# Two decoder layers on one core: the second layer's mixing gate and channel-mixing modulation are summed during the first layer's output projection and upward product

## The chip, the cores and the metric

The kernel runs on one core of one Trainium2 chip. The time is device time in microseconds of one execution, the median of the runs; lower is better. The engines of the core are TensorE (PE), VectorE (DVE), ScalarE (ACT), GpSimd (POOL) and SyncE (SP), which issues nearly all transfers. Each engine runs its own instructions in the order in which they were put, and waits for others by semaphores.

## The reference

Two layers (DEPTH = 2) over 1024 positions of width 1024, in float32. A vector `c` gives six modulation vectors per layer, 1024 long each: shift, scale and gate for token mixing, and the same for channel mixing.

```python
c_act = jax.nn.silu(c)
for l in range(DEPTH):
    mod = c_act @ ada_w[l] + ada_b[l]
    shift_m, scale_m, gate_m, shift_f, scale_f, gate_f = split(mod, 6)
    h = rms_norm(x, g_pre_mix[l]) * (1.0 + scale_m) + shift_m
    proj = h @ w_in[l] + b_in[l]
    # sliding-window attention with sinks, and a causal pooling mixer, on columns of proj
    ...
    y = concat([attention, pooled]) @ w_out[l]
    x = x + gate_m * rms_norm(y, g_post_mix[l])
    h = rms_norm(x, g_pre_ffn[l]) * (1.0 + scale_f) + shift_f
    y = (silu(h @ w_gate[l]) * (h @ w_up[l])) @ w_down[l]
    x = x + gate_f * rms_norm(y, g_post_ffn[l])
```

The change concerns `gate_m`, `scale_f` and `shift_f` of the second layer. They depend on `c` and the weights alone, so they may be worked out at any time before the second layer uses them.

## The kernel before

**Number format.** Every large product runs as three TensorE products of rounded high and low parts (`mm3`, lines L263, L266, L267; in `double` of the products by pairs the same lines). `split` makes the parts: ACT rounds (L220, high), DVE subtracts (L221, low). A matmul takes a 128x128 left operand and 512 columns. Results go to PSUM banks `acc`, of which there are four.

**Stages of a layer.** Positions are halved (512 each), and a half has four tiles of 128. Per layer: mixing (input projection, attention and pooling of both halves; in it the output projection of the first half, out0, and six first products of the channel mixing), then out1, the output projection of the second half, then `firsts[1]` (the first products of eight column pairs), then ups, and down. out0 and out1 are `natural_proj` (L664): two column halves, in each 8 k-steps of 12 matmuls, and at the end of a half four DVE products L691 that empty the four banks. The next half needs the banks again.

**ups** works through 11 pairs of columns (`up_pair`, L1137), each with products named T2, T3, T1, B22, T4 (a product for two banks is 24 matmuls). Their left operands are sums of weight quarters on DVE: L1177, L1178 (the left of T2), L1182, L1183 (the left of T3). Each bank's result is added to another by L1162 on DVE. L1099, L1196, L1198, L1200, L1207 finish the pair's SwiGLU rows. The weights come by four transfers of line L1145 per pair, on SP, two to a tile `raw`.

**Modulation jobs.** A job (`ada_sum`, L285) makes 512 numbers of a modulation vector: eight weight tiles of 128x512 (256 KB each, L306, SP) come into the buffers `ar`, of which there are two, and DVE sums them, each scaled by a column of `c_act`, into `ada` (L296 the first, L298 the other seven). The sum over partitions is then taken by PE, in one of three ways:
- `ada_gate` (L457): the sum is split into `ph` high and low parts, and two matmuls with a picking column (L469, L470) give one row of 512. DVE adds the bias and multiplies by a gain (L471, L472, in place in two `ar` buffers), and L473 stores it to DRAM; `load_gate` loads it when needed. Two jobs per sub-layer.
- `ada_pair` (L404): also split; two picking matmuls per job (L412, L413) collect four jobs in one bank of four rows, which ACT copies (L417) and PE transposes (L420); L424 adds the bias.
- `ada_columns` (L435): no split; four fp32 matmuls of the sum against a column of ones (L441) give columns at once, L446 adds the bias, L400 finishes the scale. Four jobs per sub-layer.

A job is a generator of five steps (ADA = 5): four that load two tiles each and sum the two before them, and a last one. `run(stream, steps, (other, n), ...)` steps through a main stream and takes n steps of the others spread evenly over it. Where a step of another stream stands among the main stream's instructions settles the order on each engine, within what the scheduler then moves.

**Where the jobs run before.** `ada_jobs(l)` (L1447): two gate jobs and four `ada_pair` jobs of channel mixing, in the mixing stage of the layer that uses them. The channel mixing's gate, two jobs of `ada_gate(l, 1)`, runs during ups, 14 steps over 55. The second layer's shift and scale of mixing, four `ada_columns` jobs, run during the first layer's down. out1 has no job beside it.

Of the kernel before, what the change touches and what calls it, by code (L numbers as in the profile page):

```python
# [23 lines left out]
DEPTH = 2  # L24
# [12 lines left out]
NPAIR = NFF // 2  # L37
KD = D // P
# [28 lines left out]
def hybrid_decoder_kernel(  # L67
# [367 lines left out]
    def ada_columns(l, sub, cols, ab):  # L435


        def close(r, acc):
            bank = msc_bank()
            for i in range(4):  # L440
                nc.tensor.matmul(  # L441
                    bank[:, i : i + 1], acc[:, i * P : (i + 1) * P], ones[:, 0:1], start=True, stop=True
                )
            m, o = r // 2, slice(r % 2 * 4, r % 2 * 4 + 4)
            k0 = (3 * sub + 1 - m) * KD
            nc.vector.tensor_add(ab[:, m, o], bank[:, 0:4], cols[:, k0 + o.start : k0 + o.stop])  # L446
            if m == 0:
                ada_scale(ab, sub, o, cols)

        return [  # L450
            (l, (3 * sub + 1 - r // 2) * D + r % 2 * 512, lambda acc, r=r: close(r, acc), True)
            for r in range(4)
        ]
# [3 lines left out]
    def ada_gate(l, sub):  # L457

        gates[l, sub] = row = dr.tile([1, D], F32, tag="gate", name="gate", bufs=2 * DEPTH)

        def close(half, hi, lo):
            n0 = (3 * sub + 2) * D + half * 512
            o = slice(half * 512, half * 512 + 512)
            gb = t_("ar", [P, 512])[0:1]
            gg = t_("ar", [P, 512])[0:1]
            nc.sync.dma_start(gb, ada_b[l : l + 1, n0 : n0 + 512])
            nc.sync.dma_start(gg, (g_post_ffn if sub else g_post_mix)[l : l + 1, o])
            bank = msc_bank()
            nc.tensor.matmul(bank[0:1, :], picks[:, 3:4], hi, start=True, stop=False)  # L469
            nc.tensor.matmul(bank[0:1, :], picks[:, 3:4], lo, start=False, stop=True)  # L470
            nc.vector.tensor_add(gb, bank[0:1, :], gb)  # L471
            nc.vector.tensor_mul(gb, gb, gg)  # L472
            nc.sync.dma_start(row[:, o], gb)  # L473

        return [
            (l, (3 * sub + 2) * D + half * 512, lambda hi, lo, half=half: close(half, hi, lo))
            for half in range(2)
        ]
# [6 lines left out]
    ADA = KD // 2 + 1  # L485

    def ada_stream(jobs):

        for l, n0, close, *whole in jobs:
            got = []  # L490
            yield from ada_sum(l, n0, got, *whole)
            close(*got)
# [869 lines left out]
    def layer_cols(l, rows=None):  # L1362
        return dict(cols=cols_of(rows or load_col_rows(l)), abm=t_("colp", [P, 2, KD]), abf=t_("colp", [P, 2, KD]))
# [81 lines left out]

    rotary_tables(recent["cast"])
    def ada_jobs(l):  # L1447
        return ada_stream(ada_gate(l, 0) + ada_pair(l, 1, par["cols"], par["abf"]))

    FIRST = (3, NPAIR - 3)  # L1450
    for l in range(DEPTH):
        cols = par["cols"]
# [21 lines left out]
        side = ada_jobs(l)  # L1474
# [52 lines left out]
        drain(pool)  # L1527
        xs = load_residual(1)
        fn, ss, out1 = mix_out(l, cats[1], G)
        for i, _ in enumerate(out1, 1):  # L1530
            if i == 2 * KD:
                next(firsts[1])

        def second_norm():
            yield from post_norm(1, fn, ss, xs)
# [11 lines left out]
        run(firsts[1], 2 * FIRST[1], (norm, NT + 2 + HK + 2))  # L1547
        drain(norm)

        nxt, jobs = None, []  # L1550
        if l + 1 < DEPTH:
            nxt = layer_cols(l + 1)
            jobs = ada_columns(l + 1, 0, nxt["cols"], nxt["abm"])
        side = ada_stream(ada_gate(l, 1))

        wd, load = down_loads(l)

# [5 lines left out]
                        after(load(B11, g), recent["raw"])  # L1563
                    yield

        run(ups(), 5 * NPAIR + 2 * (NPAIR - sum(FIRST)), (side, 2 * ADA + 4))
        drain(side)
        G = load_gate(l, 1)
        side = ada_stream(jobs)
# [91 lines left out]
```

## Time and profile before

| what | value |
|---|---|
| median of 3 runs | 1906.01 us (1905.44 to 1906.4) |
| the profiled execution's span | 1904.4 us |
| first layer's mixing | 50 to 309 us |
| first layer's out1, firsts[1], ups, down | 309 to 356, 356 to 437, 437 to 745, 745 to 990 us |
| second layer's mixing | 990 to 1246 us |
| second layer's out1, firsts[1], ups, down | from 1246, 1293, 1374 and 1682 us to the end |

The profile shows one execution. The times of the stages are read from the first and last instructions of their lines in the timeline. In a row of the view by windows, a number with (x...) is an engine's busy time and its instructions. In the timeline a row is start, duration, engine, line and operation, output and inputs; `[0.33 <-ACT hi L220]` is idle time of the engine just before the row, and what ended it. Rows of waits give the sum, the number and the longest.

### The profile page before, as it was taken

Reading aid. Unit: us, or ns where it says so; the run is one execution under the profiler, and the core shown is the slowest. Engines: PE = TensorE matmul, PEld = TensorE weight load, DVE = VectorE, ACT = ScalarE, POOL = GpSimd, SP = SyncE. Lnnn points to the kernel's source line nnn. Section 1 sums busy time; section 2 is a strip of 40 time slices with the busy share of each in tenths; the row PEclk is TensorE's granted clock in tenths of the full one; section 3 lists DMA queues with packets and bytes.
Section 4 is the critical chain, followed back from the end, with each engine's and each line's share of the span. In section 5 each row is a group of like instructions: output and inputs, shape, how many; then the busy total and the mean of one; then the engine's idle time right before and its main releaser. Section 6 shows DMA issues by size and latency. Waiting matters only on the chain.

```text
span 1904.4 us, 26019 instructions
## 1 busy us (share of the span) xinstructions
PE 1864.7 (98%) x8954; PEld 1540.3 (81%) x8954; DVE 1540.4 (81%) x2889; ACT 948.4 (50%) x1791; POOL 20.0 (1%) x67
## 2 busy tenths in 40 slices
PE   7999999999999999999999999999999999999998
PEld 5887788888888788888888868888887888888886
DVE  7899886668898888788879988846888888867687
ACT  4875795654222223445558667845622222234452
POOL 0000000000000000000000000000000000000000
PEclk9999999999999999999999989999999999999999
DMA  9345563655555665944554464536654565574343
GB/s 341 112 144 161 161 221 125 191 172 193 194 183 188 205 210 172 320 143 150 172 179 139 126 181 164 178 111 209 214 189 146 198 216 197 199 249 157 117 141 114
DMA packets 229540, 341.86 MB, mean 180 GB/s; under 512 B 17016, under 2 KB 126472, under 8 KB 229408
## 3 DMA queue, kind: packets, MB, share of 16 engines
q1 hardware_dynamic: 228800, 338.10, 53.8%
q10 hardware_dynamic: 576, 2.10, 0.3%
q8 instruction: 70, 1.15, 0.3%
q14 instruction: 62, 0.51, 0.1%
q0 software_dynamic: 32, 0.00, 0.0%
HBM read 267.25 MB, written 72.89 MB: 179 GB/s over the span
## 4 chain that ended last, share of the span: by engine, by line
PE 80%; DVE 10%; DMA 5%; ACT 3%; issue 2%; SPq 0%; DVEq 0%; ACTq 0%; POOL 0%; POOLq 0%
PE acc L263 25%; PE acc L266 24%; PE acc L267 24%; DMA ar<-in_ada_w_dram 2%; DVE lo L221 1%; DVE ada L298 1%; DMA raw<-in_w_up_dram 1%; PE msc L904 1%; PE msc L561 1%; ACT hi L220 1%; PE pv L263 1%; PE pv L266 1%; PE pv L267 1%; ACT raw L554 1%; DVE fn L1162 1%
## 5 line engine op out<-in xcount | busy, mean ns | idle before, releaser
L220 ACT ACTIVATE hi<-raw 128x1024 fp32r<-128x1024 f32 (+1 forms) x388 | 331.8, 868 | 360.1 <-PE acc L266 197.1
L221 DVE TENSOR_TENSOR lo<-raw,hi 128x1024 fp32r<-128x1024 f32 (+1 forms) x388 | 380.2, 987 | 121.3 <-ACT hi L220 116.4
L263 PE MATMUL acc<-t,hi 128*128 128x512 f32 x704 | 274.6, 390 | 2.7 <-ACT hi L220 2.6
L266 PE MATMUL acc<-t,hi 128*128 128x512 f32 x704 | 274.0, 389 | 0.0
L267 PE MATMUL acc<-t,lo 128*128 128x512 f32 x704 | 271.8, 389 | 0.0
L263 PE MATMUL acc<-bh,hi 128*128 128x512 f32 x520 | 202.8, 390 | 0.0
L267 PE MATMUL acc<-bh,lo 128*128 128x512 f32 x520 | 202.4, 389 | 0.0
L263 PE MATMUL acc<-hT,hi 128*128 128x512 f32 x480 | 190.2, 396 | 0.6 <-DVE fn L691 0.6
L266 PE MATMUL acc<-hT,hi 128*128 128x512 f32 x480 | 188.4, 392 | 0.0
L267 PE MATMUL acc<-hT,lo 128*128 128x512 f32 x480 | 187.6, 392 | 0.0
L1162 DVE TENSOR_TENSOR fn<-acc,fn 128x512 f32<-128x512 f32 x220 | 150.3, 685 | 38.2 <-PE acc L267 37.6
L263 PEld LDWEIGHTS acc<-t,hi 128*128 128x128 f32 x704 | 132.2, 188 | 32.1 <-ACT hi L220 5.1
L267 PEld LDWEIGHTS acc<-t,lo 128*128 128x128 f32 x704 | 132.2, 188 | 28.7 <-DVE lo L221 1.2
L266 PEld LDWEIGHTS acc<-t,hi 128*128 128x128 f32 x704 | 132.2, 188 | 27.1
L266 PE MATMUL acc<-ph,hi 128*128 128x512 f32 x320 | 124.7, 390 | 0.0
L1098 ACT ACTIVATE fn<-fn 128x512 f32<-128x512 f32 x44 | 27.9, 633 | 181.7 <-DVE fn L1162 181.7
L263 PEld LDWEIGHTS acc<-bh,hi 128*128 128x128 f32 x520 | 97.6, 188 | 20.2
L267 PEld LDWEIGHTS acc<-bh,lo 128*128 128x128 f32 x520 | 97.6, 188 | 20.2
L298 DVE SCALAR_TENSOR_TENSOR ada<-ar,c_act,ada 128x512 f32<-128x512 f32 x140 | 104.6, 747 | 10.1 <-DMA ar<-in_ada_w_dram 9.7
L263 PE MATMUL acc<-hi 128*128 128x512 f32 x256 | 103.5, 410 | 2.4 <-DVE fn L691 2.0
L263 PEld LDWEIGHTS acc<-hT,hi 128*128 128x128 f32 x480 | 90.2, 188 | 19.2 <-DVE fn L691 1.4
L267 PEld LDWEIGHTS acc<-hT,lo 128*128 128x128 f32 x480 | 90.1, 188 | 18.6 <-issue 0.2
(323 smaller groups left out, 3814.5 us busy)
## 6 DMA issues: line engine op xcount, KB each, us to landing
ar<-in_ada_w_dram SPq DMA_DIRECT2D x160, 256.0 KB
raw<-in_w_gate_dram SPq DMA_DIRECT2D x44, 512.0 KB
raw<-in_w_up_dram SPq DMA_DIRECT2D x44, 512.0 KB
raw<-in_w_in_dram SPq DMA_DIRECT2D x80, 256.0 KB
raw<-keeps SPq DMA_DIRECT2D x40, 512.0 KB
keeps<-fn SPq DMA_DIRECT2D x66, 256.0 KB
two_b<-in_w_down_dram SPq DMA_DIRECT2D x30, 512.0 KB
raw<-keepa SPq DMA_DIRECT2D x25, 512.0 KB
```

The source lines that it names most:

```text
L220: a = nc.scalar.activation(hi, src, AF.Copy)
L221: v = nc.vector.tensor_sub(lo, src, hi.bitcast(F32))
L263: ins = nc.tensor.matmul(dst, lh, rh, start=first, stop=False)
L266: nc.tensor.matmul(dst, lh, rl, start=False, stop=False)
L267: return nc.tensor.matmul(dst, ll, rh, start=False, stop=last)
L298: ins = nc.vector.scalar_tensor_tensor(acc, w, c_act[:, i : i + 1], acc, op0=ALU.mult, op1=ALU.add)
L554: nc.scalar.activation(hf, bank, AF.Identity, bias=shift, scale=scale)
L561: ins = nc.tensor.transpose(bank[:, t * P : (t + 1) * P], src[t], ident)
L904: nc.tensor.transpose(bank[:, i * P : (i + 1) * P], s[:, ii, ck * P : (ck + 1) * P], ident)
L1098: nc.scalar.activation(g, g, AF.Silu)
L1162: nc.vector.tensor_add(halves_of(dst)[m], bank, halves_of(src)[m])
```

## The change

`ada_jobs` makes no jobs for the second layer. During the first layer, the second layer's two gate jobs and four channel-mixing jobs (these as `ada_columns` instead of `ada_pair`) become one stream `ahead`. 15 of its 30 steps run beside the 16 k-steps of the first layer's out1; what is left comes in ups, ahead of the two gate jobs that were there, at 29 steps over 55 in place of 14. `layer_cols` of the second layer (bias and gain columns) moves from ahead of ups to ahead of out1.

```diff
     def ada_jobs(l):
+        if l:
+            return iter(())
         return ada_stream(ada_gate(l, 0) + ada_pair(l, 1, par["cols"], par["abf"]))
...
         fn, ss, out1 = mix_out(l, cats[1], G)
-        for i, _ in enumerate(out1, 1):
-            if i == 2 * KD:
-                next(firsts[1])
+        nxt, ahead = None, iter(())
+        if l + 1 < DEPTH:
+            nxt = layer_cols(l + 1)
+            ahead = ada_stream(ada_gate(l + 1, 0) + ada_columns(l + 1, 1, nxt["cols"], nxt["abf"]))
+
+        def out1_ahead():
+            for i, _ in enumerate(out1, 1):
+                if i == 2 * KD:
+                    next(firsts[1])
+                yield
+
+        run(out1_ahead(), 2 * KD, (ahead, 3 * ADA))
...
-        nxt, jobs = None, []
-        if l + 1 < DEPTH:
-            nxt = layer_cols(l + 1)
-            jobs = ada_columns(l + 1, 0, nxt["cols"], nxt["abm"])
-        side = ada_stream(ada_gate(l, 1))
+        jobs = ada_columns(l + 1, 0, nxt["cols"], nxt["abm"]) if nxt else []
+
+        def ups_side():
+            yield from ahead
+            yield from ada_stream(ada_gate(l, 1))
+
+        side = ups_side()
...
-        run(ups(), 5 * NPAIR + 2 * (NPAIR - sum(FIRST)), (side, 2 * ADA + 4))
+        run(ups(), 5 * NPAIR + 2 * (NPAIR - sum(FIRST)), (side, (5 if nxt else 2) * ADA + 4))
```

The order of instructions shows three places. First, DVE at the boundary between the two column halves of the first layer's out1, before:

```order
L221 TENSOR_TENSOR lo<-cfb,hi 128x512
L221 TENSOR_TENSOR lo<-raw,hi 128x512 x2
L691 TENSOR_TENSOR fn<-acc,G 128x512 x3
L221 TENSOR_TENSOR lo<-raw,hi 128x512
L691 TENSOR_TENSOR fn<-acc,G 128x512
```

and after, from the first gate job's last operations on (`ar<-msc,ar` is its bias, L296 the first tile of the second gate job):

```order
L471 TENSOR_TENSOR ar<-msc,ar 1x512
L221 TENSOR_TENSOR lo<-raw,hi 128x512
L472 TENSOR_TENSOR ar<-ar 1x512
L221 TENSOR_TENSOR lo<-raw,hi 128x512
L691 TENSOR_TENSOR fn<-acc,G 128x512 x2
L296 TENSOR_SCALAR ada<-ar,c_act 128x512
L691 TENSOR_TENSOR fn<-acc,G 128x512
L221 TENSOR_TENSOR lo<-raw,hi 128x512
L691 TENSOR_TENSOR fn<-acc,G 128x512
```

The third and the fourth L691 now stand behind a first sum that needs a loaded tile. At the end of out1 it is the same with L296 ahead of all four and an L298 between the second and the third.

Second, DVE in the second pair of the first layer's ups, from the eviction L1162 of T4's first bank (the pair before) on, before (`lo<-raw,hi` is first the split of T2's left operand, then T3's):

```order
L1162 TENSOR_TENSOR fn<-acc,fn 128x512
L1196 TENSOR_TENSOR sb<-fn,sb 128x512
L1183 TENSOR_TENSOR raw<-raw 128x8x128
L1198 TENSOR_TENSOR fn<-sb,sa 128x512
L1200 TENSOR_TENSOR fn<-sa,fn 128x512
L1162 TENSOR_TENSOR fn<-acc,fn 128x512
L221 TENSOR_TENSOR lo<-raw,hi 128x1024
L1099 TENSOR_TENSOR fn<-fn 128x512
L1162 TENSOR_TENSOR fn<-acc,fn 128x512
L1207 TENSOR_TENSOR fn<-fn 128x512
```

and after:

```order
L1162 TENSOR_TENSOR fn<-acc,fn 128x512
L1196 TENSOR_TENSOR sb<-fn,sb 128x512
L298 SCALAR_TENSOR_TENSOR ada<-ar,c_act,ada 128x512
L1198 TENSOR_TENSOR fn<-sb,sa 128x512
L1200 TENSOR_TENSOR fn<-sa,fn 128x512
L1162 TENSOR_TENSOR fn<-acc,fn 128x512
L298 SCALAR_TENSOR_TENSOR ada<-ar,c_act,ada 128x512
L1099 TENSOR_TENSOR fn<-fn 128x512
L1162 TENSOR_TENSOR fn<-acc,fn 128x512
L1207 TENSOR_TENSOR fn<-fn 128x512
L1183 TENSOR_TENSOR raw<-raw 128x8x128
L1162 TENSOR_TENSOR fn<-acc,fn 128x512
```

In these rows the first two L1162 belong to the two banks of T4 of the pair before, and the third to the first bank of this pair's T2. L1183, the sum that T3 needs, stood third and now stands behind that L1162. It is so in the second, fourth, fifth, seventh and tenth pair; in the sixth, eighth and ninth T2's own split L221 stands behind T4's second L1162. Before, L1183 stood ahead of all L1162 of T2 in every pair.

Third, SP in ups, where the weight loads of a pair (L1145) stand; before, in the third pair's loads:

```order
L1145 DMA raw<-in_w_gate_dram 128x4x256
L306 DMA ar<-in_ada_w_dram 128x512
L1145 DMA raw<-in_w_up_dram 128x4x256
L306 DMA ar<-in_ada_w_dram 128x512
L1151 DMA fn<-firsts 128x1024
L1145 DMA raw<-in_w_gate_dram 128x4x256
L1145 DMA raw<-in_w_up_dram 128x4x256
```

and after, in the loads of a pair in the middle of ups:

```order
L1145 DMA raw<-in_w_gate_dram 128x4x256
L306 DMA ar<-in_ada_w_dram 128x512
L1145 DMA raw<-in_w_up_dram 128x4x256
L306 DMA ar<-in_ada_w_dram 128x512
L1151 DMA fn<-firsts 128x1024
L1145 DMA raw<-in_w_gate_dram 128x4x256
L306 DMA ar<-in_ada_w_dram 128x512 x2
L1145 DMA raw<-in_w_up_dram 128x4x256
```

Before, two L306 at most stood among a pair's loads, and in many pairs none; now up to four do, and two or three in most pairs. In the second layer's mixing no operation of the jobs is left, and its out1, ups and down stand as before.

## The prediction

> **What bounds the kernel now.** I read the head of the page first, then TensorE's share and clock by slices.
>
> ```profile
> span 1904.4 us, 26019 instructions
> PE 1864.7 (98%) x8954; PEld 1540.3 (81%) x8954; DVE 1540.4 (81%) x2889; ACT 948.4 (50%) x1791; POOL 20.0 (1%) x67
> PEclk9999999999999999999999989999999999999999
> ```
>
> TensorE (PE) sets the end: it is busy 98% of the span, at full clock in all slices but one. So the change can gain only where PE waits or is slowed, and loses wherever it makes PE wait. That slice is the second layer's mixing. The view by windows gives the stages that the change touches: time, then busy us of PE, PEld, DVE, ACT, POOL, then PE's clock, DMA share and GB/s.
>
> ```profile
> 309.00:356.00 47.00, 46.71 (x205) 37.85 (x204) 22.81 (x35) 23.96 (x46) 0.00 (x0) 1.00 0.33 102
> 356.00:437.00 81.00, 81.00 (x375) 67.39 (x374) 60.77 (x103) 49.27 (x82) 0.00 (x0) 1.00 0.68 216
> 437.00:745.00 308.00, 306.68 (x1351) 252.36 (x1350) 260.67 (x335) 83.46 (x97) 0.00 (x0) 1.00 0.54 184
> 990.00:1095.00 105.00, 103.36 (x669) 90.33 (x668) 96.02 (x294) 76.73 (x192) 3.59 (x11) 1.00 0.43 133
> 1095.00:1150.00 55.00, 50.85 (x238) 38.88 (x236) 47.12 (x130) 33.36 (x82) 0.70 (x1) 0.91 0.60 179
> 1150.00:1230.00 80.00, 78.45 (x447) 66.31 (x447) 66.09 (x184) 68.84 (x165) 2.73 (x8) 1.00 0.52 172
> ```
>
> In order: first layer's out1, firsts[1] and ups; then second layer's mixing in three stretches, of which only the last holds no modulation work. Where the six jobs are taken from, PE idles 4.15 of 55 us and the clock is 0.91; where they are put, PE loses 0.29, 0.00 and 1.32 us. DVE is the engine to watch: in out1 it is half free (22.81 of 47), in ups it is busy 260.67 of 308.
>
> **What goes, from the second layer's mixing.** The waits of PE in the middle stretch are two of the jobs' making, and the DVE rows from there show how: each L298 adds one weight tile into a modulation sum, each L691 frees a PSUM bank of out0.
>
> ```profile
> PE msc L825 <- DVE rt L798: 1.6, 1, 1.6
> PE acc L263 <- DVE fn L691: 1.2, 2, 0.8
> ...
> 1128.88 1.28 DVE L691 TENSOR_TENSOR fn<-acc,G 128x512 f32<-128x512 f32 x2
> 1130.08 0.74 DVE L298 SCALAR_TENSOR_TENSOR ada<-ar,c_act,ada 128x512 f32<-128x512 f32 x1
> 1130.74 0.68 DVE L691 TENSOR_TENSOR fn<-acc,G 128x512 f32<-128x512 f32 x1
> 1131.35 0.75 DVE L298 SCALAR_TENSOR_TENSOR ada<-ar,c_act,ada 128x512 f32<-128x512 f32 x1
> 1132.01 0.68 DVE L691 TENSOR_TENSOR fn<-acc,G 128x512 f32<-128x512 f32 x1
> ```
>
> I price the waits against the stretch without jobs, which idles 1.55 of 80 us, 1.9%. At that share the 55 us would idle 1.1 instead of 4.15: 3.1 us. The clock of 0.91 costs 55 x 0.09 = 5.0 us of full-speed work. The stretch 990 to 1095 idles 1.6%, so nothing is to be had there. The matmuls that leave are 12: eight picks matmuls of `ada_pair` and four of `ada_gate`. Their pitch, and the four transposes:
>
> ```profile
> 531.39 0.39 PE L266 MATMUL acc<-t,hi 128*128 128x512 f32 x1
> 531.62 0.39 PE L267 MATMUL acc<-t,lo 128*128 128x512 f32 x1
> ...
> 1144.21 0.34 PE msc L420 x4
> ```
>
> Starts lie 0.23 us apart (a record's 0.39 overlaps the next), so 12 x 0.23 + 0.34 = 3.1 us. The term is **-11.2 us** (3.1 + 5.0 + 3.1). Its lower end is -5 (other waits of that stage, which the third stretch also has, take the place of half), its upper end -15 (all idle time of the first two stretches, 1.64 + 4.15, with clock 5.0 and matmuls 3.1, is 13.9, and small gaps between records on top).
>
> **What comes, in out1.** Both gate jobs and the first tiles of the third now run here, 15 steps over 16 k-steps. DVE has room: 22.81 us plus 14 L298 and 2 L296, about 10 us, in 47. Four picks matmuls arrive: 4 x 0.23 = 0.9. They stand in the middle of a k-step and wait for the split of the sum; the like waits of the pair's matmuls (L412) were these:
>
> ```profile
> its engine sat idle before it (us, times) until:
>   ACT ph L220: 0.5, 2
> ```
>
> I take 0.5 us for each of two, 1.0. At both bank boundaries of out1 the changed order puts an L296 or L298 ahead of some of the four L691, and L296 waits for its tile. A tile takes this long, by the chain of waits in the second layer:
>
> ```profile
> 1109.27 4.01 DMA ar<-in_ada_w_dram
> ...
> 1115.42 3.07 DMA ar<-in_ada_w_dram
> ```
>
> Its `ar` slot becomes free at the gate's L472, two k-steps (5.5 us) before the boundary less some 2 us for the picks, so a 4-us load lands about when L296 stands first: 0.9 us for the first boundary, 0.7 (one L298) for the second. The term is **+3.5 us**, from +1 (everything hidden, matmuls alone) to +7.5 (each boundary waits out one more load of 3 to 4 us less what has gone by). firsts[1] takes the rest of the third job, some five L298 on a DVE with 20 us to spare: **+0.5**, 0 to 2. I cost the second layer's `layer_cols`, which now stands ahead of out1, at nothing: a few small rows beside out1's DMA share of 0.33; without that cover it would be one load, 4 us.
>
> **What comes, in ups.** Four column jobs close here, on top of the two gate jobs that were here before. Where `ada_pair` made one row set for four jobs, `ada_columns` runs four fp32 matmuls per job (L441). The same line runs in the first layer's down stage:
>
> ```profile
> 786.36 0.39 PE L267 MATMUL acc<-bh,lo 128*128 128x512 f32 x1
> 786.59 0.94 PE L441 MATMUL msc<-ones_r,ada 128*128 128x1 f32 x8
> 787.40 0.49 PE L263 MATMUL acc<-bh,hi 128*128 128x512 f32 x1
> ```
>
> From 786.59 to 787.40 is 0.81 us; four jobs cost **+3.2**, with PE full on both sides of it.
>
> DVE gets 24 more tile sums (three of the four jobs) of 0.67 us, 16 us, and its idle time of 47 us covers them on average. Not in place, though. Each pair's T3 needs the sum L1183, then ACT's rounding; L1183's start to T3's start is this long in the trace:
>
> ```profile
> 531.25 1.22 DVE L1183 TENSOR_TENSOR raw<-raw 128x1024 f32<-128x1024 f32 x1
> 532.39 0.68 DVE L1207 TENSOR_TENSOR fn<-fn 128x512 f32<-128x512 f32 x1
> 532.99 0.68 DVE L1162 TENSOR_TENSOR fn<-acc,fn 128x512 f32<-128x512 f32 x1
> ...
> 532.98 0.39 PE L267 MATMUL acc<-t,lo 128*128 128x512 f32 x1
> 533.70 0.50 PE L263 MATMUL acc<-t,hi 128*128 128x512 f32 x1 [0.33 <-ACT hi L220]
> ```
>
> 2.45 us (531.25 to 533.70), and PE lost 533.70 - 532.98 - 0.23 = 0.49 there. The other pair in which a job's L298 pushed L1183 late lost 1.15:
>
> ```profile
> 642.97 0.39 PE L267 MATMUL acc<-t,lo 128*128 128x512 f32 x1
> 644.35 0.50 PE L263 MATMUL acc<-t,hi 128*128 128x512 f32 x1 [0.99 <-ACT hi L220]
> ```
>
> These two, 1.64 us, were all of it, since L1183 stood ahead of every eviction of T2. In the changed order the added operations push it further: in five of the pairs (second, fourth, fifth, seventh, tenth) L1183 stands **behind the first L1162 of T2**, and that one can't start before T2's first bank is finished. An eviction starts 0.43 us after the start of its bank's last matmul:
>
> ```profile
> 513.94 0.39 PE L267 MATMUL acc<-t,lo 128*128 128x512 f32 x1
> 514.37 0.69 DVE L1162 TENSOR_TENSOR sb<-acc,fn 128x512 f32<-128x512 f32 x1 [0.63 <-PE acc L267]
> ```
>
> So with L1162 and L1207 ahead (0.60 each, start to start) T3 starts 0.43 + 1.20 + 2.45 = 4.08 after that matmul, while PE has T2's second bank, 13 pitches, 2.96 us. PE loses 1.1; with an L298 between as well, 1.8; with L1207 gone by, 0.5. The five pairs: 1.1 + 1.8 + 1.1 + 0.5 + 1.8 = 6.3. In three other pairs (sixth, eighth, ninth) T2's own split L221 stands behind the second L1162 of T4: 0.43 + 0.60 + 1.2 for the split is 2.2 us, against 4 matmuls and one pitch, 1.1: PE loses 1.1 twice, and 2.4 in the ninth, where an L298 and L1099 stand between too. Together 4.6. The stalls are 6.3 + 4.6 = 10.9, less 1.64 before: **+9.3**. They are counted from PE's own matmuls, so a DVE that is otherwise early can't remove them; the lower bound is +6 (orders ahead with less width), the upper +12 (DVE behind from the pair before).
>
> Whether such stalls cost clock too is open. Two windows show a stall and what followed:
>
> ```profile
> 1095.00:1100.00 5.00, 3.27 (x17) 2.34 (x15) 4.92 (x20) 2.62 (x7) 0.00 (x0) 1.00 0.57 155
> 1100.00:1105.00 5.00, 4.82 (x18) 3.86 (x19) 4.45 (x10) 3.77 (x8) 0.00 (x0) 0.66 0.49 141
> ```
>
> After the 1.6-us wait the clock was 0.66 for 5 us, 1.7 us of work lost. After the 1.15-us stall in ups none was (clock 1.00 in its window). Of the three stalls of 1.8 and 2.4 us I count one as followed by a drop: **+1.7**, 0 to 5.1.
>
> Here a rule of the Trainium skill speaks otherwise ("TensorE: Matmul & The Clock Gate", "What's actually happening"): it gives the half clock only after an idle window of about 3.4 us. By it no stall here would cost clock, and the sum would be 1.7 us less; the trace disagrees, with 0.66 after a wait of 1.6 us, so I keep the term.
>
> **Sum.** -11.2 + 3.5 + 0.5 + 3.2 + 9.3 + 1.7 = +7.0 us on the execution of 1904.4. The runs' median, 1906.0, is 1.6 above the span: 1904.4 + 7.0 + 1.6 = **1913.0 us**. A measurement here can tell about 0.2%, 3.8 us, from no change: bounds 1902.2 and 1909.8.
>
> **The rivals.**
>
> *Not slower: DVE sets the pace of the whole second-layer mixing.* It is busy 96.02 of 105 and 47.12 of 55 us there, 91% and 86%, and loses this:
>
> ```profile
> 437.00:745.00 308.00, 10.44 (x14) 1.00 0.54 184
> 990.00:1230.00 240.00, 31.43 (x42) 0.98 0.50 156
> ```
>
> (L298 alone: busy and count in ups, then in the second layer's mixing.) Of 31.4 us, DVE's idle time there (8.98 + 7.88 = 16.9) already covers some, 14.5 would come off, with 3.1 of matmuls: -17.6 in place of -11.2. The clock's 1.7 may go as well: 7.0 - 6.4 - 1.7 = -1.1, **1905 us**. It decides from a relief of 14.4 us on: there the sum falls under +3.8. Against it: PE is busy 103.36 of 105 in the first stretch, so DVE isn't waited for there. It passes below 1902 only from a relief of 22. Chance 0.25, of which 0.08 below 1902.2.
>
> *Heavier: weight loads held on SP.* In ups a pair's four weight loads were issued almost free of modulation loads; now up to two L306 stand between the two halves of one tile, and L306 waits for a slot that an L298 frees. T2 starts from those loads:
>
> ```profile
> DVE raw L1177 <- DMA raw<-in_w_up_dram: 2.9, 4, 1.5
> ```
>
> Four waits, the longest 1.5 us, so the loads are not early now. If three pairs come one L306 late, a 3-us transfer less 0.5 of slack, 7.5 us are added: **1920.5 us**. For it: the order. Against it: DMA share is 0.54. Chance 0.20.
>
> *The change doesn't do what it says:* the jobs could spill past ups, where everything waits for the drain. The last L471 stands in the tenth of eleven pairs, so no; chance 0.02, at +4 for one load: 1917.
>
> **Numbers.** Forecast 0.53 at 1913.0 (1908 to 1917), not slower 0.25 at 1905, heavier 0.20 at 1920.5. Range 1901.5 to 1922.5: from the lower ends of all terms (-15 + 1 + 3.2 + 6 = -4.8, 1901.2) to the heavier rival with one more drop of the clock (1922.2). Faster by over 0.2%: 0.08. Within: 0.17 and a tenth of the forecast's own part, some 0.22 in all. Slower: 0.70.
>
> **What would show it.** PE's idle share and clock in the second layer's mixing: 1.9% and 1.00, the stage 11 us shorter. out1 of the first layer 50.5 us instead of 47, ups 322 instead of 308, with waits of PE for ACT's L220 (T3) and for DVE's L221 (T2) in eight pairs, none above 2.6 us. Long waits of L1177 for DMA would speak for the second rival, a mixing stage shorter by over 15 us for the first. The forecast is wrong if ups grows by less than 8 us.

## The result, and the profile after

The changed kernel took 1918.91 us in the median (1916.77 to 1920.1, 4 runs) beside 1906.2 for before: 1.006 times, 95% interval 1.0048 to 1.0073. It is slower, by 9 to 14 us. The page of the changed kernel, lines as shown of before:

```profile
span 1918.3 us, 26041 instructions
PE 1865.5 (97%) x8974; PEld 1540.2 (80%) x8974; DVE 1541.2 (80%) x2888; ACT 943.3 (49%) x1786; POOL 18.9 (1%) x67
PEclk9999999999999999999999999999999999999999
```

PE and DVE did the same work (1865.5 and 1541.2 us busy against 1864.7 and 1540.4) in a span 13.9 us longer, so the time went into waits. The view by windows shows where (columns as in the prediction; the stages lie up to 25 us later than in before):

```profile
309.00:360.00 51.00, 49.02 (x214) 38.70 (x213) 38.23 (x60) 25.39 (x49) 0.00 (x0) 1.00 0.61 181
360.00:441.00 81.00, 81.00 (x375) 67.34 (x374) 64.87 (x110) 48.54 (x82) 0.00 (x0) 1.00 0.75 241
441.00:769.00 328.00, 314.75 (x1382) 257.23 (x1382) 277.12 (x364) 83.31 (x97) 0.00 (x0) 0.99 0.57 192
1014.00:1119.00 105.00, 104.20 (x683) 93.07 (x683) 80.63 (x273) 76.12 (x194) 2.34 (x11) 1.00 0.22 68
1119.00:1160.00 41.00, 39.45 (x210) 32.82 (x209) 29.72 (x93) 29.35 (x73) 0.66 (x1) 1.00 0.31 99
1160.00:1242.00 82.00, 80.47 (x459) 68.08 (x458) 66.75 (x186) 70.02 (x167) 2.76 (x8) 1.00 0.52 172
```

In ups (third row) PE idles 13.25 us where it idled 1.32; the second layer's mixing (the last three rows) now runs at full clock with 3.88 us idle of 228, where 240 us held 7.34 us idle and a slow stretch.

The lengths of the stages, each from the start of one instruction to that of the next stage's like instruction (first L691 of out1, first L1177, first matmul of down, first L763, first L691 of the second layer's out1, first L1177, first matmul of down):

| stage | before | changed | jobs left out (second experiment) |
|---|---|---|---|
| to out1's first L691 | 332.0 | 333.7 | 331.3 |
| rest of out1, firsts[1] | 107.6 | 110.4 | 107.2 |
| ups | 311.5 | 331.4 | 314.4 |
| down | 234.7 | 236.7 | 236.4 |
| second layer's mixing, to out1's first L691 | 282.8 | 267.8 | 267.5 |
| rest of out1, firsts[1] | 108.6 | 107.8 | 107.6 |
| second layer's ups | 310.5 | 313.6 | 313.5 |
| second layer's down | 216.7 | 216.9 | 216.5 |

The differences add up to 13.9. Down and the second layer's ups hold the same instructions in all three, and were 2 and 3 us shorter in the one profile of before: that is the spread of single executions, and the ups of the first layer, too, hold the same instructions in the first and the third column, 2.9 us apart. What the change made is +4.5 up to the end of firsts[1], +17 to +20 in ups, and -15 in the second layer's mixing.

The waits of PE in the changed kernel's ups, and of DVE for weights (total, times, longest):

```profile
PE acc L267 <- DVE lo L221: 7.0, 3, 3.7
PE acc L263 <- ACT hi L220: 6.3, 5, 1.7
...
DVE raw L1177 <- DMA raw<-in_w_up_dram: 5.9, 6, 1.7
DVE ada L298 <- DMA ar<-in_ada_w_dram: 0.4, 1, 0.4
```

Three waits at T2 (for L221) and five at T3 (for L220), as DVE's order had it. For tiles of the modulation jobs DVE waited 0.4 us in all. The second pair, in the timeline, the engine DVE first and then PE:

```profile
482.13 0.68 DVE L1162 TENSOR_TENSOR fn<-acc,fn 128x512 f32<-128x512 f32 x1
482.73 0.68 DVE L1207 TENSOR_TENSOR fn<-fn 128x512 f32<-128x512 f32 x1
483.33 1.22 DVE L1183 TENSOR_TENSOR raw<-raw 128x1024 f32<-128x1024 f32 x1
...
483.71 0.39 PE L267 MATMUL acc<-t,lo 128*128 128x512 f32 x1
485.77 0.50 PE L263 MATMUL acc<-t,hi 128*128 128x512 f32 x1 [1.67 <-ACT hi L220]
```

T2's last matmul starts at 483.71, when L1183 has run for 0.4 us; T3 comes 2.44 us after L1183's start, and PE loses 2.06 less one pitch, 1.83.

### The profile page after: what moved, and what is told of

Its sections match the earlier page's. It is cut to its first block, busy times and chain, and to the rows that moved or that the text cites. A ratio compares the mean times of both kernels' runs of the same rounds, so it can differ in the third digit from the quotient of the medians.

```text
span 1918.3 us, 26041 instructions
## 1 busy us (share of the span) xinstructions
PE 1865.5 (97%) x8974; PEld 1540.2 (80%) x8974; DVE 1541.2 (80%) x2888; ACT 943.3 (49%) x1786; POOL 18.9 (1%) x67
## 4 chain that ended last, share of the span: by engine, by line
PE 74%; DVE 13%; DMA 6%; ACT 4%; issue 2%; SPq 0%; DVEq 0%; ACTq 0%; POOL 0%; POOLq 0%
PE acc L263 22%; PE acc L266 22%; PE acc L267 22%; DMA ar<-in_ada_w_dram 2%; DMA raw<-in_w_up_dram 2%; DVE lo L221 2%; ACT hi L220 1%; DVE ada L298 1%; PE msc L904 1%; PE msc L561 1%; DVE fn L1162 1%; PE pv L263 1%; ACT sb L888 1%; PE pv L266 1%; PE pv L267 1%
## 5 line engine op out<-in xcount | busy, mean ns | idle before, releaser
L220 ACT ACTIVATE hi<-raw 128x1024 fp32r<-128x1024 f32 (+1 forms) x388 | 331.1, 868 | 375.4 <-PE acc L266 192.7
L221 DVE TENSOR_TENSOR lo<-raw,hi 128x1024 fp32r<-128x1024 f32 (+1 forms) x388 | 380.1, 987 | 105.6 <-ACT hi L220 101.6
L263 PE MATMUL acc<-t,hi 128*128 128x512 f32 x704 | 276.9, 393 | 8.4 <-ACT hi L220 8.4
L267 PE MATMUL acc<-t,lo 128*128 128x512 f32 x704 | 272.7, 392 | 7.0 <-DVE lo L221 7.0
L263 PE MATMUL acc<-bh,hi 128*128 128x512 f32 x520 | 202.9, 390 | 0.0
L267 PE MATMUL acc<-bh,lo 128*128 128x512 f32 x520 | 202.4, 389 | 0.0
L263 PE MATMUL acc<-hT,hi 128*128 128x512 f32 x480 | 190.1, 396 | 1.0 <-DVE fn L691 1.0
L267 PE MATMUL acc<-hT,lo 128*128 128x512 f32 x480 | 187.5, 391 | 0.0
L1162 DVE TENSOR_TENSOR fn<-acc,fn 128x512 f32<-128x512 f32 x220 | 150.7, 685 | 42.8 <-PE acc L267 42.6
L263 PEld LDWEIGHTS acc<-t,hi 128*128 128x128 f32 x704 | 133.1, 189 | 39.6 <-ACT hi L220 12.5
L267 PEld LDWEIGHTS acc<-t,lo 128*128 128x128 f32 x704 | 133.1, 189 | 36.8 <-DVE lo L221 8.6
L298 DVE SCALAR_TENSOR_TENSOR ada<-ar,c_act,ada 128x512 f32<-128x512 f32 x140 | 104.7, 748 | 18.8 <-DMA ar<-in_ada_w_dram 17.8
L263 PEld LDWEIGHTS acc<-bh,hi 128*128 128x128 f32 x520 | 97.6, 188 | 20.5 <-ACT sb L1260 0.4
L267 PEld LDWEIGHTS acc<-bh,lo 128*128 128x128 f32 x520 | 97.6, 188 | 20.3
L263 PEld LDWEIGHTS acc<-hT,hi 128*128 128x128 f32 x480 | 90.2, 188 | 19.8 <-DVE fn L691 1.9
L267 PEld LDWEIGHTS acc<-hT,lo 128*128 128x128 f32 x480 | 90.1, 188 | 18.6 <-issue 0.2
L266 PEld LDWEIGHTS acc<-hT,hi 128*128 128x128 f32 x480 | 90.4, 188 | 16.6
```

Of the source, the lines that this page charges most:

```text
L220: a = nc.scalar.activation(hi, src, AF.Copy)
L221: v = nc.vector.tensor_sub(lo, src, hi.bitcast(F32))
L263: ins = nc.tensor.matmul(dst, lh, rh, start=first, stop=False)
L266: nc.tensor.matmul(dst, lh, rl, start=False, stop=False)
L267: return nc.tensor.matmul(dst, ll, rh, start=False, stop=last)
L298: ins = nc.vector.scalar_tensor_tensor(acc, w, c_act[:, i : i + 1], acc, op0=ALU.mult, op1=ALU.add)
```

## The experiments

Each ran beside the kernel before; the ratio of the runs has its 95% interval. The stalls are counted in two ways: in DVE's order as the prediction did it, and in the trace as PE's start-to-start gap less one pitch of 0.23. The experiments' line numbers can differ by one or two.

**1. The sums for T3 ahead of T2's evictions.**

```diff
         bank = times(a11, T2)
-        added(X, bank, X)
-        yield
         nc.vector.tensor_sub(a12, a12, a11)
         nc.vector.tensor_sub(a11, a22, a11)
+        added(X, bank, X)
+        yield
         bank = times(a11, T3)
```

> The changed kernel with the two sums for T3 (the lines L1182 and L1183) issued ahead of T2's evictions in every pair; all modulation work stays where the change put it. In DVE's order L1183 then stands ahead of T2's evictions in all pairs, and T2's split ahead of T4's second eviction in all but the ninth pair. Theory 'queue order' (the cost in ups is PE waiting for DVE operations that stand behind an eviction): seven of the eight stalls go, 10.6 of the 14.5 us that PE lost at them; the ninth pair's 3.9 us and the clock drop behind it stay: 1908 us (1906 to 1910), ups 317 us instead of 327. Rival 'loads' (weight loads come late behind modulation loads) and rival 'work' (what counts is how much DVE and DMA have to do in ups): no load and no operation is less, so within 2 us of the changed kernel's 1918.9.

1.0027 times before (1.0016 to 1.0038): 5 to 6 us of the changed kernel's loss (1.006, and 1.0051 in the eleventh experiment) are gone with no operation and no load less. The forecast of 1908 us was missed all the same: the median is 1914.6, and the profiled execution, 1907.9 us, was the fastest of twelve, so its trace tells the places better than the sizes. ups took 322.8 us in it, 8.6 less. PE's waits in ups:

```profile
PE acc L267 <- DVE lo L221: 4.1, 4, 2.4
PE acc L263 <- ACT hi L220: 1.4, 2, 0.8
```

13.3 us of waits became 5.5; the 2.4 is the ninth pair's, which the order kept. The rivals 'loads' and 'work' forecast no change and fall as the main cause. But 10.6 were to go, not 8: five small stalls stand where the count has none. Three of them (the other waits for L221) are at T3's split, which the fifth experiment explains. The other two, 0.9 and 0.8 us at T3's rounding in the sixth and eighth pair, come after first sums that had waited 1.9 and 1.7 us for their weights, so late loads had a part there.

**2. The jobs left out.**

```diff
-            ahead = ada_stream(ada_gate(l + 1, 0) + ada_columns(l + 1, 1, ...))
+            gates[l + 1, 0], nxt["abf"] = gates[l, 0], par["abf"]
...
-        run(ups(), ..., (side, (5 if nxt else 2) * ADA + 4))
+        run(ups(), ..., (side, 2 * ADA + 4))
```

The second layer then uses the first layer's gate and modulation, and the six jobs are left out altogether.

> The six moved jobs are left out altogether: the second layer uses the first layer's mixing gate and channel-mixing modulation. Nothing is put into out1 and ups, nothing runs in the second layer's mixing. This measures the gain alone. By the two traces the second layer's mixing became 14.2 us shorter: 1892 us (1890 to 1894). By the prediction's term of 11.2 us: 1895. If DVE set the pace of that stage as a whole (17.6 us): 1888.6.

0.9938 (0.9925 to 0.9951), 11.8 us (9.4 to 14.3) off 1908. The prediction's 11.2 holds by the runs; the single profiles give 15.0, a difference that the spread of the unchanged stages (2 to 3 us) nearly covers: the fifth experiment's trace, which has the jobs there too, had 280.8 us in the second layer's mixing, 13.3 more than with the jobs left out. What the change adds is then some 23 us (1.006 against 0.9938), where the terms of the prediction for it add up to 18.2.

**3. Only the gate jobs moved.**

```diff
-        if l:
-            return iter(())
-        return ada_stream(ada_gate(l, 0) + ada_pair(l, 1, par["cols"], par["abf"]))
+        pairs = ada_pair(l, 1, par["cols"], par["abf"])
+        return ada_stream(pairs if l else ada_gate(l, 0) + pairs)
...
-            ahead = ada_stream(ada_gate(l + 1, 0) + ada_columns(...))
+            ahead = ada_stream(ada_gate(l + 1, 0))
...
-        run(out1_ahead(), 2 * KD, (ahead, 3 * ADA))
+        run(out1_ahead(), 2 * KD, (ahead, 2 * ADA))
...
-        run(ups(), ..., (side, (5 if nxt else 2) * ADA + 4))
+        run(ups(), ..., (side, 2 * ADA + 4))
```

> Only the two gate jobs move to the first layer's out1 (10 steps beside its 16 k-steps); the four channel-mixing jobs stay in the second layer's mixing as before, now without the gates ahead of them; ups is as before. Theory 'place' (PE's waits in that mixing come where the last tiles meet out0; without the gates ahead, the four jobs are done before it): nearly all of the 14.2 us less the 2.2 us of the jobs' own matmuls, at the out1 cost of 3.5: 1898 us (1896 to 1901). Rival 'share' (the relief goes with the number of tiles taken away, 16 of 48): 14.2 / 3 = 4.7 less, 3.5 more: 1905.

1.0027 (1.0018 to 1.0036), slower than before: a miss for both. The second layer's mixing took 278.7 us, 4.1 less. The rates of the jobs in the mixing were left as they were, so the last L298 ran at 1117 us, inside out0 still, after a 1.5-us wait of PE and a fall of the clock, and the stretch is only a little cleaner (PE idles 3.1 of 55 us where it idled 4.2, the clock is 0.97 where it was 0.91):

```profile
1105.00:1160.00 55.00, 51.86 (x268) 42.65 (x267) 41.54 (x124) 37.87 (x94) 1.63 (x3) 0.97 0.34 106
```

So the run doesn't tell 'place' from 'share'. It had a cost of its own too, a 3.3-us wait of PE for an L691 at out1's end (experiment 6).

**4. Rows instead of columns.**

```diff
-ada_columns(l + 1, 1, nxt["cols"], nxt["abf"])
+ada_pair(l + 1, 1, nxt["cols"], nxt["abf"])
```

> The changed kernel with the four channel-mixing jobs as before (split, picking matmuls, a row copy and transposes) instead of fp32 matmuls against ones, at the same places. The four fp32 groups, 3.2 us of PE, go, and 2.2 us of picking matmuls and transposes come; DVE gets four splits more. Theory 'queue order': DVE's order now has five places with a stall, 7.6 us where the changed kernel's order gives 10.9 by the same count, so 4.4 us of the measured 14.5 go too, with the ninth pair's stall still there: 1913.5 us (1911 to 1916). Rival 'work': more DVE work, so 1918 to 1921.

1.0025 (1.0014 to 1.0036), 1913.2 us: as 'queue order' forecast, although DVE has four splits more to do. The trace is again of the fastest of twelve executions, 1907.4 us. PE lost 9.8 us at the five places that the count names (2.3, 0.7, 2.4, 3.1, 1.4 against 1.8, 0.5, 1.1, 2.4, 1.8) and 0.55 at the picks L469 of the tenth pair.

**5. The control: the first experiment's edit in the kernel before.**

> The control for the first experiment: the kernel before with the same two sums issued ahead of T2's evictions, modulation jobs where they were. Theory 'queue order': the edit cures what an added operation does to DVE's order; before has only about 1.6 us (two pairs of the first layer) and as much in the second layer to cure: 0 to 3 us faster than before. Rival (the edit is a gain of its own, whatever stands in ups): about 6 us faster, as the first experiment was against the changed kernel.

1.0032 (1.0019 to 1.0044): 6 us slower, a miss for both. The waits in the first layer's ups are 5.6 us at L267 for DVE's L221, where before had 1.3 us, at L263 for ACT's L220. One of them, DVE and then PE (L1162 is the eviction of T2's first bank, L221 T3's split):

```profile
534.21 0.68 DVE L1162 TENSOR_TENSOR fn<-acc,fn 128x512 f32<-128x512 f32 x1
534.80 0.68 DVE L1207 TENSOR_TENSOR fn<-fn 128x512 f32<-128x512 f32 x1
535.40 0.74 DVE L298 SCALAR_TENSOR_TENSOR ada<-ar,c_act,ada 128x512 f32<-128x512 f32 x1
536.07 1.22 DVE L221 TENSOR_TENSOR lo<-raw,hi 128x1024 fp32r<-128x1024 f32 x1
...
535.34 0.39 PE L263 MATMUL acc<-t,hi 128*128 128x512 f32 x1
537.34 0.50 PE L267 MATMUL acc<-t,lo 128*128 128x512 f32 x1 [1.61 <-DVE lo L221]
```

The same mechanism at a third place: with the sums early, T3's split stands behind the eviction, L1207 and an L298, and PE runs out of matmuls that need the high part alone. The edit cures T3's sum and opens a hole at T3's split; in the changed kernel the cure was worth more, as the first experiment's time shows. My count looked at two places of DVE's queue, and there are three.

**6. The columns in down.**

```diff
-            ahead = ada_stream(ada_gate(l + 1, 0) + ada_columns(...))
+            ahead = ada_stream(ada_gate(l + 1, 0))
...
-        run(out1_ahead(), 2 * KD, (ahead, 3 * ADA))
+        run(out1_ahead(), 2 * KD, (ahead, 2 * ADA))
...
+        jobs = ada_columns(l + 1, 0, ...) + ada_columns(l + 1, 1, nxt["cols"], nxt["abf"])
...
-        run(ups(), ..., (side, (5 if nxt else 2) * ADA + 4))
+        run(ups(), ..., (side, 2 * ADA + 4))
...
-            (between(), 7 * NPAIR), (side, 28),
+            (between(), 7 * NPAIR), (side, 52),
```

> The two gate jobs run beside the first layer's out1 as in the change (10 steps of 16); the four channel-mixing jobs, as columns, run in the first layer's down behind the four jobs that are there (52 steps over 77 instead of 28). ups stands as before. Theory 'queue order': down has no operation of the pairs' kind, PE lost nothing there beside 28 L298 and DVE is idle for 44 of 245 us; so the cost is 3.2 us of fp32 matmuls in down and about 3 in out1 and firsts, against the relief of about 12 (measured by leaving the jobs out): 5 to 7 us faster than before. Rival 'work': 28 more L298 (20 us of DVE) cost in down what they cost in ups, some 15 us: 5 to 10 us slower than before.

1.0009 (0.9994 to 1.0024), a miss for both: the 17 us or more of ups are gone, the second layer's mixing is as short as in the change (267.7), but down took 243.9 us, 7.5 more than with the jobs left out: 3.2 of fp32 matmuls, 2.0 in waits of PE that the trace shows, the rest unresolved. And out1 ended with a wait. DVE there:

```profile
356.32 0.75 DVE L298 SCALAR_TENSOR_TENSOR ada<-ar,c_act,ada 128x512 f32<-128x512 f32 x1 [2.38 <-DMA ar<-in_ada_w_dram]
356.99 1.22 DVE L221 TENSOR_TENSOR lo<-raw,hi 128x1024 fp32r<-128x1024 f32 x1
358.13 0.69 DVE L691 TENSOR_TENSOR fn<-acc,G 128x512 f32<-128x512 f32 x1
```

DVE waits 2.38 us for a tile, the eviction stands behind it, and PE waited 3.4 us for the bank. This is what the prediction's upper end of the out1 term has at each of the two boundaries, met at one, at another rate.

**7. Sums without loads.** Each of the four channel-mixing jobs loads one tile and sums it eight times, so seven of its eight loads are left out; the gate jobs load all their tiles.

```diff
-                    w = t_("ar", [P, 512])
-                    nc.sync.dma_start(w, src[:, i, n0 : n0 + 512])
+                    if i == 0 or not (whole and n0 >= 3 * D):
+                        w = t_("ar", [P, 512])
+                        nc.sync.dma_start(w, src[:, i, n0 : n0 + 512])
```

> The changed kernel, but each of the four channel-mixing jobs loads one weight tile and sums it eight times; so seven of eight loads of these jobs are left out, and all sums stay. DVE's order then has five places with a stall by the same count: fifth and seventh pair 0.5, eighth 1.1, ninth 2.4, tenth 1.8, 6.3 us. Theory 'queue order': PE waits at these places and no others, by those amounts and up to a third more, and the time falls by what the order's count falls, 4 to 6 us, to 5 to 8 us slower than before. Rival 'loads': with the loads gone the stalls go as well: ups costs only the 3.2 us of fp32 matmuls, and the kernel is about 6 us faster than before.

1.0017 (1.0003 to 1.0031), 3 us slower than before, between the two forecasts. The waits of its ups:

```profile
PE acc L267 <- DVE lo L221: 4.2, 2, 2.3
PE acc L263 <- ACT hi L220: 3.2, 3, 1.5
```

Two at T2 and three at T3, in the pairs that the count names (fifth, seventh, eighth, ninth, tenth): PE lost 1.6, 0.7, 2.1, 2.4, 1.4, 8.2 us against 6.3 counted. 'Loads', by which the kernel would be 6 us faster than before, falls. But the run shows less than it was made for, since the edit took away loads and changed DVE's order at once. From the seventh pair on, the jobs are the gate jobs, whose tiles are loaded as in the changed kernel (from 622 us on), so only the fifth pair's stall of 1.6 us stands where the loads are gone. That one shows that a stall needs no late tile.

**8. The first experiment with 31 steps.**

```diff
-(side, (5 if nxt else 2) * ADA + 4)
+(side, 31 if nxt else 2 * ADA + 4)
```

> The first experiment's kernel (sums for T3 ahead of T2's evictions) with 31 steps of modulation work over the 55 of ups instead of 29, so that no pair's T2 split stands behind T4's second eviction any more. By the count in DVE's order no stall is left. Theory 'queue order': the ninth pair's 2.5 us and what clock it costs go: 2 to 4 us faster than the first experiment's kernel, about even with before. Rival 'work': the same as the first experiment, 5 us slower than before.

1.001 (0.9996 to 1.0024), 3 us faster than the first experiment, as forecast, though the two intervals overlap. PE still lost 5.9 us in seven stalls that the count doesn't see, the longest 1.7 us, in an execution that was the slowest of eleven.

**9 and 10. One column job beside out1 and three in down; the gates at the change's rate and four columns in down.**

```diff
-            ahead = ada_stream(ada_gate(l + 1, 0) + ada_columns(l + 1, 1, nxt["cols"], nxt["abf"]))
+            cj = ada_columns(l + 1, 1, nxt["cols"], nxt["abf"])
+            ahead = ada_stream(ada_gate(l + 1, 0) + cj[:1])
...
-        jobs = ada_columns(l + 1, 0, nxt["cols"], nxt["abm"]) if nxt else []
+        jobs = ada_columns(l + 1, 0, nxt["cols"], nxt["abm"]) + cj[1:] if nxt else []
...
-        run(ups(), ..., (side, (5 if nxt else 2) * ADA + 4))
+        run(ups(), ..., (side, 2 * ADA + 4))
...
-            (between(), 7 * NPAIR), (side, 28),
+            (between(), 7 * NPAIR), (side, 48),
```

The tenth differs from the sixth in one line:

```diff
-        run(out1_ahead(), 2 * KD, (ahead, 2 * ADA))
+        run(out1_ahead(), 2 * KD, (ahead, 3 * ADA))
```

> As in the change, 15 steps of modulation work beside the first layer's out1: the two gate jobs and the first channel-mixing job. The other three channel-mixing jobs run in the first layer's down (48 steps over 77) instead of ups, whose jobs and steps are as before. Theory 'queue order': ups costs nothing extra but the first job's fp32 matmuls (0.8); out1 and firsts cost 3 as in the change, without the 3.4-us wait that the sixth experiment had at out1's end; down costs 3/4 of the 7.5 us that it cost there, 5.6; against 12 of relief: 1 to 4 us faster than before. Rival 'work' (the sum of modulation work costs the same wherever it stands beside full PE): as the sixth experiment, 1 to 2 us slower than before.

> The sixth experiment with the gate jobs' ten steps at the change's rate (15 over 16), so that they end three quarters through out1; four channel-mixing jobs in down as there. Theory 'queue order': the sixth experiment's 3.4-us wait at out1's end (an L691 behind an L298 whose tile was late by 2.4 us) goes, the rest stays: 2 to 3 us faster than the sixth, so 0 to 2 us faster than before. Rival (the two-buffer ring sets how long 16 tiles take, and the wait moves to the boundary in the middle): no difference to the sixth experiment.

0.9994 (0.9981 to 1.0006) and 0.9995 (0.9983 to 1.0007): no change from before, and neither run tells its two forecasts apart by the time. In the tenth the wait at out1's end is 0.34 us instead of 3.39, and the ratio is 0.14% better than the sixth's, as forecast, with intervals that overlap; down took 245.8 us (242.1 in the ninth), so beside down the jobs cost about what their absence brings.

**11. The changed kernel again.**

> The changed kernel itself, on the chip and beside the runs of before that the last runs of the study had, for a common base: 8 to 14 us slower than before (its first comparison: 1.0048 to 1.0073 times). In the profile the same eight pairs of ups stall, as its order has it: T3 in the second, fourth, fifth, seventh and tenth, T2 in the sixth, eighth and ninth. A place that doesn't stall again would speak against the theory 'queue order'.

1.0051 (1.0034 to 1.0067). All eight pairs stall again and no other:

| pair | 2 | 4 | 5 | 6 | 7 | 8 | 9 | 10 | sum |
|---|---|---|---|---|---|---|---|---|---|
| counted in DVE's order, us | 1.1 | 1.8 | 1.1 | 1.1 | 0.5 | 1.1 | 2.4 | 1.8 | 10.9 |
| lost in the changed kernel's trace | 1.8 | 1.8 | 1.1 | 1.6 | 0.9 | 2.0 | 3.9 | 1.4 | 14.5 |
| lost in this run's trace | 2.1 | 2.1 | 1.1 | 1.6 | 2.3 | 1.9 | 2.4 | 1.4 | 14.9 |

**12. Half of the jobs.**

```diff
+        if l:
+            return ada_stream(ada_columns(l, 1, par["cols"], par["abf"])[1:])
...
+            ahead = ada_stream(ada_gate(l + 1, 0) + ada_columns(...)[:1])   # 15 steps beside out1, ups as before
```

> Half of the work moves: the two gate jobs and the first channel-mixing job (24 tiles of 48) run beside the first layer's out1 as in the change; the other three channel-mixing jobs, as columns, stay in the second layer's mixing; ups and down as before. Theory 'share' (from the third experiment: the relief goes with the tiles taken away, 4 us for 16): 24 of 48 tiles, 6 us of relief, at 3 to 4 us in out1, firsts and ups: 1 to 4 us faster than before. Rival 'place' (only the tiles that meet out0 cost): the last tiles are still there, so no relief beyond 2 us: 1 to 3 us slower than before.

0.9985 (0.9975 to 0.9995): 3 us faster than before, as 'share' forecast, and the only version with all of the work in it that beats both kernels. The second layer's mixing took 273.5 us, 9.3 less, with half of the tiles still in it:

```profile
994.00:1099.00 105.00, 102.31 (x668) 90.14 (x668) 92.62 (x288) 74.40 (x188) 2.08 (x9) 1.00 0.41 130
1099.00:1150.00 51.00, 48.98 (x272) 41.28 (x271) 35.57 (x114) 35.58 (x90) 1.08 (x3) 1.00 0.27 87
```

Its last job's matmuls stand at 1092 us, before out0. 'Share' gave 6 us of relief; the traces give 9.3, or 7.3 beside the fifth experiment's 280.8 us, so whether place counts as well stays open. The stretch of out0 is clean (clock 1.00, 2.0 us idle), while PE idles 2.7 us in the stretch that has the jobs, where before had 1.6.

## Why the prediction came out as it did

**Direction and size.** Forecast slower, 1913.0 with a range of 1901.5 to 1922.5; 1918.9 was measured, a loss of 12.7 us where 7.0 were forecast (10.3 in the eleventh experiment's runs). The mechanism of the forecast, stalls where DVE's queue puts a needed operation behind an eviction, was the cause: the places were right pair by pair, in the changed kernel and in its repeat, and other orders of DVE moved the places and the time (experiments 1, 4 and 5). The stalls (12.9 us for 9.3) and the clock (2.8 for 1.7) came out larger in the trace than their terms, 4.7 of the 5.7 us by which the forecast was short.

**The second layer's mixing, -11.2.** 11.8 by leaving the jobs out (interval 9.4 to 14.3), 15.0 in the traces of before and changed. Right by the runs. The first rival, a relief of 17.6 with DVE as the pace of the stage, fell by them too.

**out1 and firsts, +3.5 and +0.5.** 4.5 in the table, of which about 1 stood there before out1 began. PE waited 1.2 us for a split at the second gate's picks and 0.7 us for L691 at the end, of the kind and size priced. Right; that the end can cost 3.4 instead was seen in experiments 3 and 6.

**The fp32 matmuls, +3.2.** The four groups stand in the trace, in ups, with 0.8 us each (455.79 to 456.60 us the first). Right.

**The stalls, +9.3: the term that was mis-sized.** They measured 14.5 less 1.64, +12.9, above the term's own upper end of 12. The step that failed is "0.43 + 0.60 + 1.2 for the split is 2.2 us": it lets T4's second eviction start as soon as its bank is ready. In the ninth pair of the changed kernel, DVE and then PE:

```profile
682.31 0.67 DVE L1162 TENSOR_TENSOR fn<-acc,fn 128x512 f32<-128x512 f32 x1
682.91 0.67 DVE L1198 TENSOR_TENSOR fn<-sb,sa 128x512 f32<-128x512 f32 x1
683.51 0.67 DVE L1200 TENSOR_TENSOR fn<-sa,fn 128x512 f32<-128x512 f32 x1
684.11 0.67 DVE L1162 TENSOR_TENSOR fn<-acc,fn 128x512 f32<-128x512 f32 x1
684.71 0.73 DVE L298 SCALAR_TENSOR_TENSOR ada<-ar,c_act,ada 128x512 f32<-128x512 f32 x1
685.37 0.67 DVE L1099 TENSOR_TENSOR fn<-fn 128x512 f32<-128x512 f32 x1
685.97 1.21 DVE L221 TENSOR_TENSOR lo<-raw,hi 128x1024 fp32r<-128x1024 f32 x1
...
683.15 0.39 PE L266 MATMUL acc<-t,hi 128*128 128x512 f32 x1
687.23 0.80 PE L267 MATMUL acc<-t,lo 128*128 128x512 f32 x1 [3.69 <-DVE lo L221]
```

T4's last matmul started four pitches before 683.15, at 682.25, so its eviction could have started at 682.68; it started at 684.11, because L1198 and L1200 stood ahead of it and DVE was behind. These 1.4 us are the difference between the 2.4 counted and the 3.85 lost, and the 3.7-us wait goes beyond the 2.6 us that the prediction gave as the longest. By the same reckoning the evictions ahead of the stalls of the second, sixth and eighth pair started 0.7, 0.4 and 0.8 us after their banks were ready, and these pairs lost 0.7, 0.5 and 0.9 us more than counted. In the ninth, DVE was behind since the pair's first sum had waited for its weights:

```profile
675.50 1.23 DVE L1177 TENSOR_TENSOR raw<-raw 128x1024 f32<-128x1024 f32 x1 [1.73 <-DMA raw<-in_w_up_dram]
```

So the second rival, late weight loads, was real in the ninth pair, with 1.4 us (the pair lost 2.4 in the repeat and in the seventh experiment, where its first sum had not waited), and may be in the eighth, whose first sum waited 1.3 us. It was not three pairs with 7.5, and that SP held the loads back behind L306 isn't shown. That the measured time lies near the rival's 1920.5 doesn't make it the cause.

**The clock, +1.7.** The 3.7-us wait came with this; PE's last matmul record ahead of it ends at 683.54:

```profile
682.51:685.93 3.42, 1.03 (x5) 0.53 (x3) 3.42 (x6) 0.63 (x1) 0.00 (x0) 1.00 0.84 287
685.93:689.34 3.41, 2.11 (x5) 1.74 (x6) 2.98 (x4) 0.31 (x1) 0.00 (x0) 0.50 0.94 311
687.23:695.00 7.77, 7.77 (x23) 6.24 (x24) 4.49 (x6) 2.50 (x3) 0.00 (x0) 0.64 0.28 103
```

From the end of the wait to 695 us the clock is 0.64, 7.77 x 0.36 = 2.8 us of work; the part of the slow time that lay inside the wait cost nothing more. After the stalls of 1.8 to 2.0 the clock stayed at 1.00. One drop, as counted, of 1.6 times the size. The rule of the Trainium skill ("TensorE: Matmul & The Clock Gate", "What's actually happening"), half clock only after an idle window of about 3.4 us, isn't borne out in this kernel either, although the wait was longer than that: the clock was at 0.50 from 685.93 on, when PE had been idle for 2.4 us. The last section has a fall after a shorter wait.

Together: 12.9 + 3.2 + 2.8 = 18.9 us, beside the 17.0 to 19.9 by which ups grew (against the second experiment's trace and that of before).

## What to carry to other kernels

An engine that is idle 15% of a stage on average still has no room where another engine waits on it in order: before adding work to its queue, list the operations that the bound engine needs next, and see whether the added ones push any of them behind an operation that itself waits for the bound engine. The instruction order tells the places; the sizes need the engine's backlog at that moment too. A place without such hand-overs isn't free either: beside down the four column jobs cost 7.5 and 9.4 us. Half of the work moved beside out1, the rest left where it was, was worth more here than all of it moved.

## What the runs showed of the hardware that was not expected

The same wait can cost clock or not. In the repeat of the changed kernel PE waited 2.27 us in the ninth pair, and so it did in the seventh experiment; the windows of the stall and of the 5 us after it, first of the repeat, then of the seventh experiment:

```profile
685.00:690.00 5.00, 2.73 (x12) 1.95 (x12) 4.79 (x8) 0.63 (x1) 0.00 (x0) 1.00 0.92 293
690.00:695.00 5.00, 5.00 (x16) 3.92 (x16) 3.12 (x4) 2.00 (x2) 0.00 (x0) 0.66 0.35 127
```

```profile
678.00:683.00 5.00, 2.73 (x13) 1.93 (x12) 4.90 (x7) 0.00 (x0) 0.00 (x0) 1.00 0.92 321
683.00:688.00 5.00, 5.00 (x24) 4.14 (x23) 4.08 (x7) 3.07 (x3) 0.00 (x0) 1.00 0.21 61
```

The clock fell to 0.66 in the one and stayed at 1.00 in the other, after equal waits well below 3.4 us. What differs is how the wait lies in time. In each of the fourteen traces the clock falls to 0.50, and within a trace the falls begin whole multiples of 3.41 us apart (before: 9, 274 and 283 of them after the first, at 165.4 us) and last one such stretch or two. Cut into these stretches, the two executions read, in the same order:

```profile
684.26:687.68 3.42, 3.21 (x15) 2.32 (x13) 3.21 (x6) 0.63 (x1) 0.00 (x0) 1.00 0.74 246
687.68:691.09 3.41, 1.34 (x6) 1.12 (x7) 3.41 (x5) 0.00 (x0) 0.00 (x0) 1.00 0.88 275
691.09:694.51 3.42, 3.42 (x10) 2.65 (x9) 1.54 (x3) 2.00 (x2) 0.00 (x0) 0.50 0.26 98
```

```profile
677.42:680.83 3.41, 1.77 (x8) 1.13 (x6) 3.31 (x6) 0.26 (x1) 0.00 (x0) 1.00 0.94 330
680.83:684.24 3.41, 2.78 (x12) 2.33 (x13) 2.49 (x4) 0.98 (x2) 0.00 (x0) 1.00 0.73 260
684.24:687.66 3.42, 3.42 (x17) 2.83 (x16) 3.42 (x5) 2.09 (x3) 0.00 (x0) 1.00 0.05 11
```

In the repeat nearly the whole wait lies in one stretch and leaves PE busy for 1.34 of 3.41 us; in the seventh experiment two stretches share it, with 1.77 and 2.78 us busy. Leaving out the first 60 and the last 20 us of each trace, each of the eleven stretches with PE busy under 45% was followed by a fall, none above 62% was, and in between some were. No run shifted a stall within its stretch, so this is read from the traces and not tested.
